# Attention scores as two products of 64 rows side by side, one PSUM bank per head

## The chip, the cores and the metric

The kernel runs on one core of a Trainium2 chip. The metric is device time in microseconds for one execution. On the core, TensorE (PE) multiplies matrices into PSUM, which has eight banks of 512 fp32 columns by 128 partitions; VectorE (DVE), ScalarE (ACT) and GpSimd (POOL) work element by element; transfers are issued from SyncE (SP). The stationary operand of a product is loaded by an instruction of its own (a row of PEld in the profile), then the other operand is streamed through the array (a row of PE).

## The reference

One decoder layer on 256 tokens of width 1024, in fp32. One input projection gives q, k and v for 16 heads of width 64. Heads 0 to 7 are stick-breaking attention, heads 8 to 15 a softmax attention on dilated windows with a bias by distance:

```python
z = jnp.einsum('bhqd,bhkd->bhqk', q_blk, k) * scale        # stick-breaking
log_stay = jnp.where(mask, jax.nn.log_sigmoid(-z), 0.0)
after = lax.cumsum(log_stay, axis=3, reverse=True) - log_stay
w = jnp.where(mask, jnp.exp(jax.nn.log_sigmoid(z) + after), 0.0)
...
sc = jnp.einsum('bhqd,bhqjd->bhqj', q_blk, k_g) * scale    # dilated, three window patterns
sc = sc - slopes_f * dist
p = jnp.exp(sc - m)
```

Each head's output is RMS-normalised with a gain, all heads go through an output projection, then residual and layer norm, a SwiGLU feed-forward part of width 2816, and residual and layer norm again.

## The kernel before

Every fp32 operand of a large product is split into two parts of fp32r, a rounded one (hi) and the rest (lo), by a copy on ScalarE and a subtraction on VectorE; `prod` (L139) forms a product of two split operands as three products, hi hi, hi lo and lo hi, into the same PSUM columns. Weights come in chunks of 1 MB and are split piece by piece (`Weights`, L66; the lines of the copy and of the subtraction are L62 and L63).

The heads are worked in eight pairs j, 0 to 3 stick-breaking, 4 to 7 dilated. `qk_step` projects q and k of a pair transposed, so that the two heads of a pair lie in partitions 0 to 63 and 64 to 127 of one PSUM bank p, q in columns 0 to 255 and k in columns 256 to 511. A pair then runs through these steps (`attend`, L369):

- `evacuate` (L181) brings q and k to SBUF, scaled and split. One of them, q for a stick-breaking pair and k for a dilated one, is padded: 512 columns, of which the first 256 hold head 0 in partitions 0 to 63 and the last 256 head 1 in partitions 64 to 127, with zeros elsewhere. So a product over all 128 rows gives both heads beside each other. The zeros are written once, on GpSimd (L175, L176). Six instructions: two copies and two subtractions of half the partitions for the padded operand (L194, L195), and one of each for the plain one (L197, L198).
- `stick_scores` (L208) computes the transposed scores: keys 0 to 127 against all queries in bank z0 (512 columns, both heads), keys 128 to 255 against queries 128 to 255 in bank z1 (256 columns), three products each, and adds the causal mask by one bf16 product a bank (L217, L218). ScalarE and VectorE form the softplus of the scores in 768 columns and split it (sph, spl).
- `stick_weights` (L233) adds the reverse cumulative sum as products of sph and spl with a triangle (negtri) and with ones (negones), six products at L239, and ScalarE takes the exponential in two instructions (L242 of 512 columns, L243 of 256).
- `dilated_scores` (L248) computes the scores of queries 0 to 127 in s0 (256 columns, both heads) and of queries 128 to 255 in s1 (512 columns), three products each; VectorE adds the bias and takes the maximum (L266), ScalarE the exponential with its sum (L269), VectorE divides.
- `dilated_weights` (L277) transposes them, six products of 128 columns (L281 to L284), and brings 512 columns to SBUF on ScalarE (L287) and 256 on VectorE (L288).
- `values` (L291) multiplies with v in plain fp32. Each head's output has 64 partitions, head 0 in 0 to 63 and head 1 in 64 to 127 of one bank, so these products use 64 columns of the array each. In the trace each of them shows as two passes; those at L298 have 256 columns, those at L303 128.
- `normalise` (L312).

TensorE's program order is written out by `Order` (L332): a clock in estimated microseconds advances with each product with weights (`fill`), each step is due a fixed delay after the step before it (`LAG_A`, `LAG_B`) and has an estimated cost (1.2 for stick-breaking scores, 0.97 for dilated ones), and is put between the products when its time has come. The framework's scheduler orders the instructions of each engine after that by its own estimate of when operands are ready, and can put products of one step apart. PSUM is held as pairs of banks under the names in, big, sml and o.

After the attention come the output projection and the first layer norm, until 140 us, and then the feed-forward part, whose products fill the rest.

## Time and profile before

| | us |
|---|---|
| median of 3 runs | 325.23 |
| lowest and highest run | 324.73 and 325.82 |
| span of the profiled execution | 324.6 |
| TensorE busy in it | 309.9 |
| VectorE, ScalarE busy | 204.7, 177.3 |

The span goes from the first to the last instruction of one profiled execution. The page gives no other time of it; the median of the runs is 0.6 us above the span. Products are pipelined: a PE row's length holds the way through the array too, so rows overlap, and the distance between the starts of two rows is what the first of them takes of the engine. A time in square brackets at a row's end is the engine's idle time before it, with what ended it.

### The profile page before, as it was taken

How to read it: one execution, taken by the hardware profiler on the slowest of the kernel's cores; microseconds unless marked ns; L12 is line 12 of the kernel's file. 1: busy time of each engine (PE TensorE's matmuls, PEld its weight loads, DVE VectorE, ACT ScalarE, POOL GpSimd, SP SyncE). 2: the span in 40 equal slices, each digit the busy share in tenths (PEclk: the TensorE clock that was granted, in tenths of full speed). 3: DMA queues.
4: the chain of work that ended last, by engine and by line, in shares of the span. 5: the costliest groups of instructions: out<-in, count | busy, mean ns of one | idle time of the engine just before them, and what ended most of it. 6: DMA issues, size and time to landing. Idle time of an engine off the chain costs nothing.

```text
span 324.6 us, 5469 instructions
## 1 busy us (share of the span) xinstructions
PE 309.9 (95%) x2168; PEld 283.6 (87%) x2168; DVE 204.7 (63%) x400; ACT 177.3 (55%) x376; POOL 10.6 (3%) x27
## 2 busy tenths in 40 slices
PE   5799999999999999999999999999999999999990
PEld 5688898799997778999999999999999988888890
DVE  3768889867888469997636456464644635250444
ACT  5669899777886547665546364453635543330000
POOL 2010000000000001200000000000000000000102
PEclk9999999999999999999999999999999999999996
DMA  6997876658532203399555464554546365000011
GB/s 182 339 405 280 319 242 239 239 206 333 193 123 73 112 2 129 112 351 383 194 169 221 140 239 142 212 178 164 226 137 240 143 214 175 2 0 0 0 67 65
DMA packets 10809, 58.35 MB, mean 180 GB/s; under 512 B 1312, under 2 KB 2336, under 8 KB 4512
## 3 DMA queue, kind: packets, MB, share of 16 engines
q1 hardware_dynamic: 10784, 58.01, 48.7%
q8 instruction: 17, 0.28, 0.3%
q14 instruction: 8, 0.07, 0.1%
HBM read 56.95 MB, written 1.05 MB: 179 GB/s over the span
## 4 chain that ended last, share of the span: by engine, by line
PE 89%; ACT 3%; DMA 2%; DVE 2%; POOL 1%; SPq 1%; issue 1%; DVEq 0%; POOLq 0%; ACTq 0%
PE pg L142 12%; PE pg L143 12%; PE pg L141 12%; PE p_in L141 7%; PE p_in L143 6%; PE p_in L142 6%; PE d L141 6%; PE d L142 6%; PE d L143 6%; DMA wraw<-in_wqk 2%; PE acc L143 2%; PE acc L141 2%; ACT whi L62 2%; PE acc L142 2%; PE o L298 2%; PE z L239 1%
## 5 line engine op out<-in xcount | busy, mean ns | idle before, releaser
L63 DVE TENSOR_TENSOR wlo<-wraw,whi 128x512 fp32r<-128x512 f32 (+2 forms) x178 | 127.5, 741 | 75.2 <-ACT whi L62 74.8
L62 ACT ACTIVATE whi<-wraw 128x512 fp32r<-128x512 f32 (+2 forms) x178 | 112.8, 668 | 79.5 <-PE pg L142 47.9
L141 PE MATMUL pg<-xhi,whi 128*128 128x256 f32 x304 | 85.5, 281 | 0.0
L143 PE MATMUL pg<-xhi,wlo 128*128 128x256 f32 x304 | 85.4, 281 | 0.0
L142 PE MATMUL pg<-xlo,whi 128*128 128x256 f32 x304 | 85.4, 281 | 0.0
L142 PEld LDWEIGHTS pg<-xlo,whi 128*128 128x128 f32 x304 | 57.4, 189 | 0.0
L141 PEld LDWEIGHTS pg<-xhi,whi 128*128 128x128 f32 x304 | 57.3, 189 | 0.0
L143 PEld LDWEIGHTS pg<-xhi,wlo 128*128 128x128 f32 x304 | 57.3, 189 | 0.0
L141 PE MATMUL p_in<-xhi,whi 128*128 128x256 f32 x128 | 37.2, 293 | 5.4 <-ACT whi L62 5.4
L142 PE MATMUL d<-wlo,a 128*128 128x512 f32 (+1 forms) x110 | 38.3, 348 | 0.0
L141 PE MATMUL d<-whi,a 128*128 128x512 f32 (+1 forms) x110 | 38.3, 348 | 0.0
L143 PE MATMUL d<-whi,a 128*128 128x512 f32 (+1 forms) x110 | 38.2, 348 | 0.0
L143 PE MATMUL p_in<-xhi,wlo 128*128 128x256 f32 x128 | 36.7, 288 | 0.3 <-DVE wlo L63 0.2
L142 PE MATMUL p_in<-xlo,whi 128*128 128x256 f32 x128 | 36.5, 288 | 0.0
L141 PEld LDWEIGHTS p_in<-xhi,whi 128*128 128x128 f32 x128 | 24.9, 195 | 6.7 <-ACT whi L62 5.8
L143 PEld LDWEIGHTS p_in<-xhi,wlo 128*128 128x128 f32 x128 | 24.9, 195 | 0.7 <-DVE wlo L63 0.7
L142 PEld LDWEIGHTS p_in<-xlo,whi 128*128 128x128 f32 x128 | 24.9, 195 | 0.3 <-issue 0.2
L141 PEld LDWEIGHTS d<-whi,a 128*128 128x128 f32 x110 | 20.7, 188 | 2.9
L142 PEld LDWEIGHTS d<-wlo,a 128*128 128x128 f32 x110 | 20.8, 189 | 2.9
L143 PEld LDWEIGHTS d<-whi,a 128*128 128x128 f32 x110 | 20.7, 188 | 2.9
L471 ACT ACTIVATE rs<-mv,eps_ln 128x1 f32<-128x1 f32 x4 | 1.1, 287 | 26.5 <-DVE mv L469 26.5
L141 PE MATMUL pg<-whi,xhi 128*128 128x256 f32 x48 | 13.8, 288 | 0.0
(123 smaller groups left out, 429.0 us busy)
## 6 DMA issues: line engine op xcount, KB each, us to landing
wraw<-in_wgu SPq DMA_DIRECT2D x22, 1024.0 KB, 4.9
wraw<-in_wd SPq DMA_DIRECT2D x11, 1024.0 KB, 4.8
wraw<-in_wqk SPq DMA_DIRECT2D x6, 1024.0 KB, 5.0
wraw<-in_wo SPq DMA_DIRECT2D x4, 1024.0 KB, 4.8
wraw<-in_wv SPq DMA_DIRECT2D x3, 1024.0 KB, 6.6
rows<-in_lnrows SPq DMA_DIRECT2D x2, 1024.0 KB, 5.7
wraw<-in_wqk SPq DMA_DIRECT2D x6, 256.0 KB, 6.6
wraw<-in_wv SPq DMA_DIRECT2D x2, 512.0 KB, 5.8
```

Of the source, the lines that this page charges most:

```text
L62: nc.scalar.activation(hi, src, AF.Copy)
L63: nc.vector.tensor_sub(lo, src, hi)
L141: nc.tensor.matmul(dst, lhs[0], rhs[0], start=start, stop=False, skip_group_check=True)
L142: nc.tensor.matmul(dst, lhs[0], rhs[1], start=False, stop=False, skip_group_check=True)
L143: nc.tensor.matmul(dst, lhs[1], rhs[0], start=False, stop=stop, skip_group_check=True)
L239: nc.tensor.matmul(dst, lhs, rhs, start=False, stop=True, skip_group_check=True)
L298: nc.tensor.matmul(o[r, 0:256], vt[g, 0][:, c], w0[:, h * 256:h * 256 + 256], start=True, stop=False, skip_group_check=True)
L471: nc.scalar.activation(r[:, 0:1], mv[:, 1:2], AF.Ln, bias=eps_ln)
```

## The change

The padded operands and their zeros go. `evacuate` copies q of both heads and k of both heads into one tile of 512 columns (oh, the rest in ol), two copies and two subtractions. The new `by_head` forms the scores of each head from its own 64 partitions, three products (hi hi, hi lo, lo hi) for each of two pieces of columns, the two heads in turn, each into a bank of its own: head 0 into a bank of big, head 1 into one of sml. A bank holds 384 columns: for a stick-breaking head 256 for keys 0 to 127 and 128 for keys 128 to 255, for a dilated head 128 for queries 0 to 127 and 256 for queries 128 to 255. So the products of the scores have 256 and 128 columns where they had 512 and 256. What follows goes by head: the mask is one product a bank on columns 0 to 127 and 256 to 383; `stick_weights` has products of 384 and 128 columns, eight where there were six; the exponentials and the copies of w have 384 columns each; `dilated_scores` goes through one head after the other; `values` reads w by head. The cost of a score step in the order is 1.0 where it was 1.2, and 0.77 where it was 0.97. The lines that are left out change comments alone.

```diff
     nc.gpsimd.tensor_copy(negones, cs[:, 2, :])
     nc.gpsimd.tensor_copy(blkr, blk)
 
-    # per pair: one operand keeps its two heads in separate columns, zero elsewhere
-    padded = []
-    for i in range(2):
-        ph = at.tile([128, 512], F32R, name=f"padhi{i}", bufs=1)
-        pl = at.tile([128, 512], F32R, name=f"padlo{i}", bufs=1)
-        nc.gpsimd.memset(ph.bitcast(F32), 0.0)
-        nc.gpsimd.memset(pl.bitcast(F32), 0.0)
-        padded.append((ph, pl))
-
     mixed = {}
 
     def evacuate(j, p):
-        a_kind = j < 4
-        ph, pl = padded[j % 2]
-        oh = at.tile([128, S], F32R, tag="oh", name="oh")
-        ol = at.tile([128, S], F32R, tag="ol", name="ol")
-        qs = slice(0, 256)
-        ks = slice(256, 512)
-        pc, oc = (qs, ks) if a_kind else (ks, qs)
-        pscale, oscale = (SCALE, 1.0) if a_kind else (1.0, SCALE)
-        for h in range(2):
-            r = slice(h * 64, h * 64 + 64)
-            c = slice(h * 256, h * 256 + 256)
-            nc.scalar.activation(ph[r, c], p[r, pc], AF.Copy, scale=pscale)
-            nc.vector.scalar_tensor_tensor(pl[r, c], p[r, pc], pscale, ph[r, c],
-                                           op0=ALU.mult, op1=ALU.subtract)
-        nc.scalar.activation(oh, p[:, oc], AF.Copy, scale=oscale)
-        nc.vector.scalar_tensor_tensor(ol, p[:, oc], oscale, oh, op0=ALU.mult, op1=ALU.subtract)
-        return (ph, pl), (oh, ol)
-
-    def heads(t, n):
-        return t[:, :2 * n].rearrange("p (h n) -> p h n", h=2)
-
-    def second(t):
-        return t.rearrange("p (h n) -> p h n", h=2)[:, :, 128:256]
-
-    def stick_scores(j, pad, plain):
-        ph, pl = pad
-        oh, ol = plain
-        z0 = bank("big", "z0")
-        z1 = bank("sml", "z1")
-        prod(z0, (oh[:, 0:128], ol[:, 0:128]), (ph, pl), True, True)
-        prod(heads(z1, 128), (oh[:, 128:256], ol[:, 128:256]), (second(ph), second(pl)), True, True)
+        oh = at.tile([128, 512], F32R, tag="oh", name="oh")
+        ol = at.tile([128, 512], F32R, tag="ol", name="ol")
+        for c, scale in ((slice(0, 256), SCALE), (slice(256, 512), 1.0)):
+            nc.scalar.activation(oh[:, c], p[:, c], AF.Copy, scale=scale)
+            nc.vector.scalar_tensor_tensor(ol[:, c], p[:, c], scale, oh[:, c], op0=ALU.mult, op1=ALU.subtract)
+        return oh, ol
+    def by_head(banks, oh, ol, pieces):
+        for dst, lhs, rhs in pieces:
+            for i, (a, b) in enumerate(((oh, oh), (oh, ol), (ol, oh))):
+                for h in range(2):
+                    r = slice(h * 64, h * 64 + 64)
+                    nc.tensor.matmul(banks[h][:, dst], a[r, lhs], b[r, rhs],
+                                     start=dst.start == 0 and i == 0, stop=i == 2, skip_group_check=True)
+    Q, K = 0, 256
+    def stick_scores(j, oh, ol):
+        z = bank("big", "z0"), bank("sml", "z1")
+        by_head(z, oh, ol, ((slice(0, 256), slice(K, K + 128), slice(Q, Q + 256)),
+                            (slice(256, 384), slice(K + 128, K + 256), slice(Q + 128, Q + 256))))
         mb = maskb[:, None, :].to_broadcast([128, 2, 128])
-        z0d = z0.rearrange("p (h n) -> p h n", h=2)
-        nc.tensor.matmul(z0d[:, :, 0:128], identb, mb, start=False, stop=True, skip_group_check=True)
-        nc.tensor.matmul(heads(z1, 128), identb, mb, start=False, stop=True, skip_group_check=True)
         sph = sk.tile([128, 768], F32R, tag="sph", name="sph")
         spl = sk.tile([128, 768], F32R, tag="spl", name="spl")
         ab = at.tile([128, 768], F32, tag="ab", name="ab")
-        parts = ((z0, slice(0, 512), 512), (z1, slice(512, 768), 256))
-        for z, c, n in parts:
-            nc.scalar.activation(ab[:, c], z[:, :n], AF.Abs)
+        for h in range(2):
+            diagonal = z[h].rearrange("p (a n) -> p a n", n=128)[:, 0:3:2, :]
+            nc.tensor.matmul(diagonal, identb, mb, start=False, stop=True, skip_group_check=True)
+        cols = slice(0, 384), slice(384, 768)
+        for h in range(2):
+            nc.scalar.activation(ab[:, cols[h]], z[h][:, :384], AF.Abs)
         nc.scalar.activation(ab, ab, AF.Exp, scale=-1.0)
         nc.scalar.activation(ab, ab, AF.Ln, bias=1.0)
-        for z, c, n in parts:
-            nc.vector.scalar_tensor_tensor(ab[:, c], z[:, :n], 0.0, ab[:, c], op0=ALU.max, op1=ALU.add)
+        for h in range(2):
+            nc.vector.scalar_tensor_tensor(ab[:, cols[h]], z[h][:, :384], 0.0, ab[:, cols[h]],
+                                           op0=ALU.max, op1=ALU.add)
         nc.vector.tensor_copy(sph, ab)
         nc.vector.tensor_sub(spl, ab, sph)
-        return z0, z1, sph, spl
-
-    def stick_weights(z0, z1, sph, spl):
-        z0d = z0.rearrange("p (h n) -> p h n", h=2)
+        return z, sph, spl
+    def stick_weights(z, sph, spl):
         for sp in (sph, spl):
-            s1 = sp[:, 512:768]
-            for dst, lhs, rhs in ((z0, negtri, sp[:, 0:512]), (z0d[:, :, 128:256], negones, heads(s1, 128)),
-                                  (z1[:, :256], negtri, s1)):
-                nc.tensor.matmul(dst, lhs, rhs, start=False, stop=True, skip_group_check=True)
-        w0 = at.tile([128, 512], F32, tag="w0", name="w0")
-        w1 = at.tile([128, 256], F32, tag="w1", name="w1")
-        nc.scalar.activation(w0, z0, AF.Exp)
-        nc.scalar.activation(w1, z1[:, :256], AF.Exp)
-        return w0, w1
+            for h in range(2):
+                s = sp[:, h * 384:h * 384 + 384]
+                nc.tensor.matmul(z[h][:, :384], negtri, s, start=False, stop=True, skip_group_check=True)
+                nc.tensor.matmul(z[h][:, 128:256], negones, s[:, 256:384], start=False, stop=True,
+                                 skip_group_check=True)
+        w = []
+        for h in range(2):
+            w.append(at.tile([128, 384], F32, tag=f"w{h}", name=f"w{h}"))
+            nc.scalar.activation(w[h], z[h][:, :384], AF.Exp)
+        return w
 
     bias_sb = at.tile([128, 8, 256], F32, name="bias_sb", bufs=1)
 
-    def dilated_scores(j, pad, plain):
-        ph, pl = pad
-        oh, ol = plain
-        s0 = bank("sml", "s0")
-        s1 = bank("big", "s1")
-        php = ph.rearrange("p (h n) -> p h n", h=2)
-        plp = pl.rearrange("p (h n) -> p h n", h=2)
-        prod(heads(s0, 128), (oh[:, 0:128], ol[:, 0:128]),
-             (php[:, :, 0:128], plp[:, :, 0:128]), True, True)
-        prod(s1, (oh[:, 128:256], ol[:, 128:256]), (ph, pl), True, True)
+    def dilated_scores(j, oh, ol):
+        s = bank("big", "s0"), bank("sml", "s1")
+        by_head(s, oh, ol, ((slice(0, 128), slice(Q, Q + 128), slice(K, K + 128)),
+                            (slice(128, 384), slice(Q + 128, Q + 256), slice(K, K + 256))))
         e = at.tile([128, 768], F32, tag="ab", name="e")
-        e0, e1 = e[:, 0:256], e[:, 256:768]
         st = at.tile([128, 4, 3], F32, tag="st", name="st")
-        for b, (sc, e, n) in enumerate(((s0, e0, 128), (s1, e1, 256))):
-            for h in range(2):
-                c = slice(h * n, h * n + n)
-                i = 2 * b + h
-                hd = 2 * (j - 4) + h
+        for h in range(2):
+            hd = 2 * (j - 4) + h
+            for b, (o, n) in enumerate(((0, 128), (128, 256))):
+                c = slice(h * 384 + o, h * 384 + o + n)
+                i = 2 * h + b
                 nc.vector.tensor_tensor_reduce(
-                    e[:, c], sc[:, c], bias_sb[:, hd, 256 - n:256], -1.0, 3.0e38,
+                    e[:, c], s[h][:, o:o + n], bias_sb[:, hd, 256 - n:256], -1.0, 3.0e38,
                     ALU.add, ALU.min, st[:, i, 0:1])
                 nc.scalar.activation(e[:, c], e[:, c], AF.Exp, bias=st[:, i, 0:1], scale=-1.0,
                                      accum_out=st[:, i, 1:2])
-            nc.vector.reciprocal(st[:, 2 * b:2 * b + 2, 2:3], st[:, 2 * b:2 * b + 2, 1:2])
-            for h in range(2):
-                c = slice(h * n, h * n + n)
-                nc.vector.tensor_scalar(e[:, c], e[:, c], st[:, 2 * b + h, 2:3], None, op0=ALU.mult)
-        return e0, e1
-
-    def dilated_weights(e0, e1):
-        t0 = bank("big", "t0")
-        t1 = bank("sml", "t1")
-        for h in range(2):
-            nc.tensor.transpose(t0[:, h * 256:h * 256 + 128], e0[:, h * 128:h * 128 + 128], ident)
-        for h in range(2):
-            nc.tensor.transpose(t0[:, h * 256 + 128:h * 256 + 256], e1[:, h * 256:h * 256 + 128], ident)
-            nc.tensor.transpose(t1[:, h * 128:h * 128 + 128], e1[:, h * 256 + 128:h * 256 + 256], ident)
-        w0 = at.tile([128, 512], F32, tag="w0", name="w0")
-        w1 = at.tile([128, 256], F32, tag="w1", name="w1")
-        nc.scalar.activation(w0, t0, AF.Copy)
-        nc.vector.tensor_copy(w1, t1[:, :256])
-        return w0, w1
-
-    def values(j, w0, w1):
+            nc.vector.reciprocal(st[:, 2 * h:2 * h + 2, 2:3], st[:, 2 * h:2 * h + 2, 1:2])
+            for b, (o, n) in enumerate(((0, 128), (128, 256))):
+                c = slice(h * 384 + o, h * 384 + o + n)
+                nc.vector.tensor_scalar(e[:, c], e[:, c], st[:, 2 * h + b, 2:3], None, op0=ALU.mult)
+        return e
+    def dilated_weights(e):
+        w = []
+        for h in range(2):
+            t = bank(("big", "sml")[h], f"t{h}")
+            for i in range(3):
+                c = slice(h * 384 + i * 128, h * 384 + i * 128 + 128)
+                nc.tensor.transpose(t[:, i * 128:i * 128 + 128], e[:, c], ident)
+            w.append(at.tile([128, 384], F32, tag=f"w{h}", name=f"w{h}"))
+            if h == 0:
+                nc.scalar.activation(w[h], t[:, :384], AF.Copy)
+            else:
+                nc.vector.tensor_copy(w[h], t[:, :384])
+        return w
+    def values(j, w):
         g, pj = divmod(j, 4)
         o = bank("o", "o")
         for h in range(2):
             c = slice(pj * 128 + h * 64, pj * 128 + h * 64 + 64)
             r = slice(h * 64, h * 64 + 64)
-            nc.tensor.matmul(o[r, 0:256], vt[g, 0][:, c], w0[:, h * 256:h * 256 + 256],
+            nc.tensor.matmul(o[r, 0:256], vt[g, 0][:, c], w[h][:, 0:256],
                              start=True, stop=False, skip_group_check=True)
         for h in range(2):
             c = slice(pj * 128 + h * 64, pj * 128 + h * 64 + 64)
             r = slice(h * 64, h * 64 + 64)
-            nc.tensor.matmul(o[r, 128:256], vt[g, 1][:, c], w1[:, h * 128:h * 128 + 128],
+            nc.tensor.matmul(o[r, 128:256], vt[g, 1][:, c], w[h][:, 256:384],
                              start=False, stop=True, skip_group_check=True)
         sq = at.tile([128, S], F32, tag="sq", name="sq")
         nc.scalar.activation(sq, o[:, :S], AF.Square)
...
     od = Order()
 
     def attend(j, p):
         a_kind = j < 4
-        pad, plain = evacuate(j, p)
+        oh, ol = evacuate(j, p)
         scores, weigh = (stick_scores, stick_weights) if a_kind else (dilated_scores, dilated_weights)
         lags = LAG_A if a_kind else LAG_B
 
         def step1():
-            x1 = scores(j, pad, plain)
+            x1 = scores(j, oh, ol)
 
             def step2():
-                x2 = weigh(*x1)
+                x2 = weigh(*x1) if a_kind else weigh(x1)
 
                 def step3():
-                    x3 = values(j, *x2)
+                    x3 = values(j, x2)
                     od.after(lags[3], 0.43, lambda: normalise(j, *x3))
                 od.after(lags[2], 0.68, step3, lambda: v_at.get(j // 4, 1e9) <= od.now)
             od.after(lags[1], 0.9 if a_kind else 0.65, step2)
-        od.after(lags[0], 1.2 if a_kind else 0.97, step1)
+        od.after(lags[0], 1.0 if a_kind else 0.77, step1)
 
     vt, v_at = {}, {}
 
```

## Rows read from the trace of the kernel before

**Rows 1.** The page's first part: busy time, share of the span, instructions.
```profile
PE 309.9 (95%) x2168; PEld 283.6 (87%) x2168; DVE 204.7 (63%) x400; ACT 177.3 (55%) x376; POOL 10.6 (3%) x27
```

**Rows 2.** Busy time by stretch: stretch, its length, each engine, clock, DMA.
```profile
17.00:45.00 28.00, 27.72 (x171) 23.19 (x170) 22.10 (x39) 24.02 (x51) 0.67 (x3) 1.00 0.85 317
...
140.00:312.00 172.00, 172.00 (x1264) 163.35 (x1263) 91.50 (x152) 73.88 (x139) 1.74 (x3) 1.00 0.45 164
```

**Rows 3.** Instructions in order of time, TensorE, scores of pair 3: start, length.
```profile
56.92 0.40 PE L141 MATMUL z<-padhi,oh 128*128 128x512 f32 x1
...
57.62 0.27 PE L141 MATMUL z<-padhi,oh 128*128 128x256 f32 x1
57.73 0.28 PE L142 MATMUL z<-padlo,oh 128*128 128x256 f32 x1
...
57.97 0.28 PE L217 MATMUL z<-maskb,identb 128*128 128x256 bf16 x1
```

**Rows 4.** The same view, stick weights of pair 2, first product and what follows.
```profile
61.00 0.40 PE L239 MATMUL z<-sph,negtri 128*128 128x512 f32 x1
...
61.95 0.39 PE L141 MATMUL p_in<-whi,xhi 128*128 128x512 f32 x1
```

**Rows 5.** The same view, value products of pair 1 and their neighbours.
```profile
40.71 0.28 PE L143 MATMUL p_in<-xhi,wlo 128*128 128x256 f32 x1
40.83 0.28 PE L141 MATMUL p_in<-xhi,whi 128*128 128x256 f32 x1
41.04 0.65 PE L298 MATMUL o<-w,v 128*64 128x256 f32 x4
41.52 0.39 PE L303 MATMUL o<-w,v 128*64 128x128 f32 x4
41.84 0.39 PE L142 MATMUL p_in<-xlo,whi 128*128 128x256 f32 x1
42.07 0.28 PE L143 MATMUL p_in<-xhi,wlo 128*128 128x256 f32 x1
```

**Rows 6.** The same view, weight loads behind those value products and at a mask.
```profile
41.84 0.19 PEld L142 LDWEIGHTS p_in<-xlo,whi 128*128 128x128 f32 x1 [0.17 <-issue]
41.95 0.19 PEld L143 LDWEIGHTS p_in<-xhi,wlo 128*128 128x128 f32 x1
...
57.97 0.10 PEld L217 LDWEIGHTS <-identb 128*128 128x128 bf16 x1
```

**Rows 7.** The same view, ScalarE, VectorE and TensorE at pair 0's evacuation.
```profile
17.93 0.38 ACT L194 ACTIVATE padhi<-p_in 64x256 fp32r<-64x256 f32 x1 [2.09 <-PE p_in L143]
18.87 0.38 ACT L194 ACTIVATE padhi<-p_in 64x256 fp32r<-64x256 f32 x1 [0.56 <-DVE padlo L195]
19.93 0.38 ACT L197 ACTIVATE oh<-p_in 128x256 fp32r<-128x256 f32 x1
...
18.42 0.42 DVE L195 SCALAR_TENSOR_TENSOR padlo<-p_in,padhi 64x256 fp32r<-64x256 f32 x1 [1.85 <-ACT padhi L194]
...
19.90 0.28 PE L143 MATMUL p_in<-xhi,wlo 128*128 128x256 f32 x1
20.46 0.47 PE L141 MATMUL z<-padhi,oh 128*128 128x512 f32 x1 [0.28 <-ACT oh L197]
```

**Rows 8.** The same view, w and value products of pair 6, scores of pair 7.
```profile
100.75 0.60 ACT L287 ACTIVATE w<-t 128x512 f32<-128x512 f32 x1
...
101.22 0.42 DVE L288 COPY w<-t 128x256 f32<-128x256 f32 x1
...
101.41 0.65 PE L298 MATMUL o<-w,v 128*64 128x256 f32 x4 [0.21 <-ACT w L287]
101.89 0.38 PE L303 MATMUL o<-w,v 128*64 128x128 f32 x2
102.20 0.39 PE L141 MATMUL s<-padhi,oh 128*128 128x256 f32 x1
...
104.40 0.51 PE L143 MATMUL s<-padhi,ol 128*128 128x256 f32 x2
```

## The prediction

> **What bounds the kernel now.** I read the busy line first, then the busy time by stretch, then TensorE's instructions in order of time, then the other engines where TensorE waits. TensorE is busy 95% of the span [rows 1]. By stretch it is busy 27.72 of 28.00 us from 17 to 45 and 172.00 of 172.00 from 140 to 312, at the full clock; VectorE and ScalarE are near their limit only early (22.10 and 24.02 of 28.00) and have half their time free later [rows 2]. So from 17 us on the end is set by how long TensorE's stream of products takes: a microsecond taken from it is a microsecond of the span, and what VectorE or ScalarE lose counts only where TensorE stands and waits for them. The 17 us ahead of that are arrival and splitting of inputs, which the change doesn't touch.
>
> **What a product costs.** A busy PE row isn't its price; the distance from start to start is. In the scores of pair 3 three products of 512 columns start at 56.92 and end their turn at 57.62, 0.233 each; those of 256 follow every 0.117 [rows 3]. That is 0.456 ns a column, with each weight load under the product before it.
>
> **Scores (by_head).** Before, a pair has three products of 512 and three of 256: 56.92 to 57.97, 1.05 us [rows 3]. Afterwards there are twelve instructions, two beside each other in six steps: three of 256 columns and three of 128. If the halves of the array run side by side, streaming is 3 x 0.117 + 3 x 0.058 = 0.53, half of before. That they do has one near case in the trace: the value products split the array by columns. Both heads' four last passes take 41.52 to 41.84, 0.32 [rows 5]; in pair 6 one head's two passes alone take 101.89 to 102.20, 0.31 [rows 8]. The second head costs nothing. I take this for the split by rows too.
>
> The same rows show the toll. From the last full product ahead of the value products to their first is 0.21 (40.83 to 41.04), where 0.117 is usual: 0.09 lost [rows 5]. On the way back the last passes of 0.107 each would be over at 41.73, yet the next product starts at 41.84, and the one behind it 0.23 later instead of 0.117: another 0.10 and 0.11. The weight loads say why: with nothing to hide under, two loads of 128 columns start at 41.84 and 41.95, 0.108 apart [rows 6]. So entering costs 0.09 and one bare load, 0.108; leaving costs 0.10 and one bare load. Behind stick-breaking scores comes the mask, whose bf16 load is half as long (0.10 against 0.19 [rows 6]), so I take 0.05 there.
>
> The Trainium skill (TensorEngine Tiling (Array Packing), Key Properties) says that a change of tiling mode drains TensorE, in whichever direction the array is split. That is what the rows show for the split by columns; if it did not hold by rows, the third rival below would be the result.
>
> A short step doesn't reach 0.058. The next pair of weights (64 rows, 128 columns) must be in place, and the only bare loads of 128 columns are 0.108 apart. No row has a load of 64 rows: from below it is 0.05 (half the elements), from above 0.108; I take 0.108, the row with as many columns, and with the start some 0.115. The Trainium skill (TensorE: Matmul & The Clock Gate, LDWEIGHTS (loading the stationary operand)) states that a load's time follows the columns and not the rows, 128 / 1.2 = 107 ns by its formula; the 0.108 agrees for the full height. By the opposite reading, loads by elements, the fourth rival is the result. From far above, a step of 128 columns costs as much as an fp32 one, two passes of 0.107: 0.21.
>
> Sum of a pair: 0.09 + 0.108 + 3 x 0.117 + 2 x 0.115 + 0.058 + 0.10 = 0.94, with the load on leaving 1.05 for a dilated pair and 0.99 for a stick-breaking one. Before 1.05: a gain of 0 and of 0.06. Over four pairs of each kind **-0.25 us** for a halved stream.
>
> **Stick weights.** Before, six products of 2048 columns in all: 61.00 to 61.95, 0.95 us [rows 4]. Afterwards eight, four of 384 and four of 128 at full height, in turn with two different weights. Columns are the same, but under a product of 128 (0.058) the next load of 0.108 has no room: four steps of 0.115 and four of 0.175 are 1.16, 0.21 more. Over four pairs **+0.85 us** (from below 0, from above 4 x (0.21 - 0.058) x 4 = +2.4). Mask, transposes and value products keep their columns.
>
> **Evacuation.** Six instructions become four: one ScalarE copy of some 0.38 and one VectorE subtraction of some 0.43 go, in each of 8 pairs. Most of it lies under TensorE's stream and is worth nothing; where TensorE waited it counts. For pair 0 the chain runs ScalarE 17.93, VectorE 18.42, ScalarE 18.87 and, last, ScalarE 19.93, and the scores start at 20.46, where the product before them, started at 19.90, left off at 20.02 [rows 7]. With q and k of both heads in one copy each, the second copy ends near 19.25 and its rest near 19.71, before 20.02. **-0.44 us**, from below 0 where TensorE's order keeps another wait there. The four cleared buffers on GpSimd go too; the inputs hadn't landed then, so nothing.
>
> **Evacuating w, and splits of a step.** w is now 384 columns on each engine where it was 512 and 256, and both heads' first value products need it: the head-1 product now waits for VectorE's copy, or in a stick-breaking pair for ScalarE's second. Behind that product in TensorE's queue stand all later products. For most pairs both copies end before it. In pair 6 TensorE already waits 0.21 for ScalarE's (started at 100.75) and begins at 101.41, while VectorE's starts at 101.22 and at some 0.55 would end near 101.77 [rows 8]. ScalarE's ends 0.12 earlier, head 1 starts up to 0.36 later: **+0.1**, between -0.1 and +0.4. Second, the order puts products of a step apart when a part comes late: pair 7 starts its scores at 102.20 and brings the last products at 104.40 [rows 8]. That was free; now each extra visit costs the toll of about 0.35. The shorter evacuation makes such splits rarer, pair 1 in the crowded start may keep one: **+0.3**, between 0 and +1.
>
> The order's cost for a score step falls by 0.2, so its estimated time runs ahead of the real one by more than before. Delays are counted from the end of a step and filled with the same products, so I take nothing; a shift of one product, 0.1 to 0.2, is its bound either way.
>
> **Sum.** -0.25 + 0.85 - 0.44 + 0.1 + 0.3 = +0.56 us, on a span of 324.6. The runs give 325.23 as median, 0.6 over the profiled span, between 324.73 and 325.82; the same distance kept, the changed kernel stands at 325.8.
>
> **Rivals.**
> First, slower: a product of 128 columns costs as much as the fp32 one, 0.21. For: the groups of instructions by shape hold no product of two fp32r parts under 256 columns, so its price is open upwards. Against: operand and instruction are the same as at 256. It is 0.35 more for each of 8 score steps (2 x 0.1 + 0.15) and 1.5 more over the stick weights: +4.3, 330.1 us. It decides from a distance of about 0.14 on.
> Second, slower too, the change doesn't do what it says: the halves load or run one after the other. Then six steps of 0.23 and the toll: +0.7 a pair, 331.4. Against it the two heads of the value products [rows 5, 8].
> Third, faster: the split by rows needs no drain and its loads are hidden. The toll of 0.41 (dilated) and 0.35 goes: -3.0, 322.8 us. For it: no row has this split. Against: the toll stands at each of the value steps. The Trainium skill (TensorEngine Tiling (Array Packing), Theoretical Speedup) gives up to twice the rate for half the rows; no run here shows it, and this is the rival that comes nearest.
> Fourth, faster: short loads by elements, so short steps at 0.06, but the toll stays. Scores save another 8 x 0.16 (two steps and the bare load), and if loads of full height also hide better than I think the weights lose nothing, -0.85: 323.7 us.
>
> **How the numbers follow.** What this kernel's runs can tell from no change is about 0.3%, 1 us. Forecast 0.42 (its own range 324.6 to 327.0, so 0.34 within, 0.06 slower, 0.02 faster); first rival 0.14; second 0.08; third 0.19; fourth 0.17, of which 0.13 faster and 0.04 within. Faster 0.34, within 0.38, slower 0.28. The range goes from the third to the first rival, 322.8 to 330.1, and leaves out the second and some of the third.
>
> **What would show it.** Right: the two heads' score products start within a few ns of each other; the first of a step comes 0.2 after the product before; steps of 128 stand about 0.115 apart; eight stick-weight products take 1.16; no gap at 20.02. Wrong: steps of 128 at 0.06 or at 0.21, the heads 0.117 apart, or a first score product 0.117 behind its predecessor. A TensorE gap at the value products of a dilated pair would be a wait that I priced too low.

## The result, and the profile after

The changed kernel takes 327.95 us (median of nine runs, 326.29 to 329.34) against 325.32 us (nine runs, 324.73 to 328.31): a ratio of 1.0067, 95% interval 1.0041 to 1.0093. Repeated, it was 327.17 against 325.88, 1.0044 (1.0023 to 1.0065). So it is slower by about half a per cent. The forecast was 325.8 in 322.8 to 330.1: the time lies in the range, but above the 324.6 to 327.0 that the forecast gave to its own case, and "slower" had only 0.28. In some executions of either kernel TensorE has half its clock for 3.4 us early on (last section), some 2 us longer; of the runs with a mean granted clock of 0.991 or more the medians are 326.89 (17 runs) and 325.34 (66, one execution of 784 us left out), 1.55 us apart.

The profiled executions hide this: both spans are 324.6 us. Wherever an execution has both on record, its time stands 1.7 to 2.1 us above its span. So 324.6 belongs to some 326.5 us: for the kernel before more than any of the three runs that the forecast started from, for the changed kernel the second lowest of nine (326.51). The 0.6 us that the forecast kept between span and median lie between different executions; as it adds its difference to the median, its 325.8 doesn't depend on them. The busy line and the windows of the changed kernel, to be set beside [rows 1, 2], say no more: TensorE is full, VectorE and ScalarE lost work that nobody waited for.
```profile
PE 310.2 (96%) x2224; PEld 283.1 (87%) x2224; DVE 201.2 (62%) x392; ACT 173.0 (53%) x368; POOL 8.7 (3%) x23
```
```profile
17.00:45.00 28.00, 27.68 (x182) 22.66 (x181) 22.66 (x40) 24.74 (x52) 0.92 (x4) 1.00 0.90 340
140.00:312.00 172.00, 172.00 (x1274) 163.34 (x1273) 92.66 (x154) 74.19 (x140) 1.74 (x3) 1.00 0.47 167
```
What to look at is the second count: in the same 172 us the changed kernel runs 1274 products, the one before 1264, and nothing of that stage was edited. Cut at the starts of products that both kernels have, three profiles of each (us):

| stretch | before | changed | difference |
|---|---|---|---|
| last projection product of 256 columns ahead of pair 0's scores to pair 4's first score | 58.43 to 58.48 | 59.60 to 59.70 | +1.2 |
| from there to the first feed-forward product by channel | 68.46 to 68.48 | 68.46 to 68.51 | 0.0 |
| from there to the first product of the down projection | 108.43 to 108.45 | 107.27 | -1.2 |
| from there to the end | 69.38 to 69.40 | 69.40 to 69.41 | 0.0 |

The stick-breaking pairs lose 1.2 us, the dilated pairs nothing on balance, and in these profiles the feed-forward stage gives back as much by a pace of its own (last section).

The edited operations are much as forecast. Scores of pair 3 in TensorE's order of time (start, length; x2 are the two heads), answering [rows 3]:
```profile
57.10 0.40 PE L143 MATMUL p_in<-whi,xlo 128*128 128x512 f32 x1
57.42 0.39 PE L187 MATMUL z<-oh 64*128 64x256 f32 x2
57.65 0.28 PE L187 MATMUL z<-ol,oh 64*128 64x256 f32 x2
57.77 0.28 PE L187 MATMUL z<-oh,ol 64*128 64x256 f32 x2
57.88 0.23 PE L187 MATMUL z<-oh 64*128 64x128 f32 x2
57.94 0.28 PE L187 MATMUL z<-ol,oh 64*128 64x128 f32 x2
58.05 0.28 PE L187 MATMUL z<-oh,ol 64*128 64x128 f32 x2
58.27 0.39 PE L203 MATMUL z<-maskb,identb 128*128 128x256 bf16 x2
58.41 0.48 PE L141 MATMUL p_in<-whi,xhi 128*128 128x512 f32 x1
```
The heads share a step; the way in costs 0.09 (57.10 + 0.23 to 57.42), the second step comes 0.23 behind the first, and a step of 256 columns takes 0.117. Of the steps of 128 the first takes 0.06 (57.88 to 57.94), the second 0.11 (57.94 to 58.05), and 0.21 pass between the last step and the mask. The weight loads of these steps start 0.11 to 0.12 apart, the bare ones at the head of the visit (57.42, 57.53) and those of the short steps (57.77 to 57.99):
```profile
57.42 0.19 PEld L187 LDWEIGHTS z<-oh 64*128 64x128 f32 x2 [0.37 <-issue]
57.53 0.19 PEld L187 LDWEIGHTS z<-ol,oh 64*128 64x128 f32 x2
...
57.77 0.19 PEld L187 LDWEIGHTS z<-oh 64*128 64x128 f32 x2
57.88 0.20 PEld L187 LDWEIGHTS z<-ol,oh 64*128 64x128 f32 x2
57.99 0.20 PEld L187 LDWEIGHTS z<-oh,ol 64*128 64x128 f32 x2
```
From the second step on, each load starts while the step ahead of its own runs, and never less than 0.11 behind the load before. So the first short step can end with its columns, and the next one takes 0.11: the price of a short product falls on the product behind it. Stick weights of pair 2, answering [rows 4], show the same. They take 61.30 to 62.39, 1.09 us. Each product of 128 columns takes 0.06, a product of 384 takes 0.17 at the head of the run and 0.23 behind one of 128, and the projection product behind the run takes 0.29 (62.39 to 62.69):
```profile
61.30 0.33 PE L220 MATMUL z<-sph,negtri 128*128 128x384 f32 x1
61.47 0.22 PE L221 MATMUL z<-sph,negones 128*128 128x128 f32 x1
61.53 0.39 PE L220 MATMUL z<-sph,negtri 128*128 128x384 f32 x1
61.76 0.22 PE L221 MATMUL z<-sph,negones 128*128 128x128 f32 x1
61.82 0.39 PE L220 MATMUL z<-spl,negtri 128*128 128x384 f32 x1
...
62.33 0.22 PE L221 MATMUL z<-spl,negones 128*128 128x128 f32 x1
62.39 0.45 PE L141 MATMUL p_in<-whi,xhi 128*128 128x512 f32 x1
62.69 0.39 PE L142 MATMUL p_in<-wlo,xhi 128*128 128x512 f32 x1
```
In the kernel before, the product behind the run takes 0.23, from 61.95 [rows 4] to
```profile
62.17 0.40 PE L142 MATMUL p_in<-wlo,xhi 128*128 128x512 f32 x1
```
What the forecast priced too low is in the extracts that follow. Pair 0's scores come in four visits, each with its own way in and out; the gap of [rows 7] is gone, but the first visit is for one product:
```profile
19.93 0.40 PE L141 MATMUL p_in<-whi,xhi 128*128 128x512 f32 x1
20.25 0.38 PE L187 MATMUL z<-oh 64*128 64x256 f32 x1
20.57 0.50 PE L142 MATMUL p_in<-wlo,xhi 128*128 128x512 f32 x1
20.90 0.40 PE L143 MATMUL p_in<-whi,xlo 128*128 128x512 f32 x1
```
From 19.93 to 20.57 is 0.64 where a product of 512 takes 0.23, and the one behind it takes 0.33: 0.51 for one score product. All operands of pair 0 had been in place since 19.46, the end of VectorE's second subtraction, so it is the order made ahead of the run that splits this step, and not a late operand:
```profile
19.04 0.42 DVE L178 SCALAR_TENSOR_TENSOR ol<-p_in,oh 128x256 fp32r<-128x256 f32 x1 [0.45 <-ACT oh L177]
```
And pair 7, answering [rows 8]: ScalarE's second copy waits its turn behind two weight splits, TensorE stands, and the visit is broken off after two products:
```profile
100.34 0.37 ACT L177 ACTIVATE oh<-p_in 128x256 fp32r<-128x256 f32 x1
100.60 1.15 ACT L62 ACTIVATE whi<-wraw 128x512 fp32r<-128x512 f32 x2
101.74 0.38 ACT L177 ACTIVATE oh<-p_in 128x256 fp32r<-128x256 f32 x1
```
```profile
101.04 0.49 PE L293 MATMUL o<-sqh,blkr 128*128 128x256 f32 x2
102.18 0.33 PE L187 MATMUL s<-oh 64*128 64x128 f32 x2 [0.65 <-ACT oh L177]
102.70 0.50 PE L141 MATMUL acc<-whi,mh 128*128 128x512 f32 x1 [0.19 <-DVE ol L178]
...
104.26 0.33 PE L187 MATMUL s<-ol,oh 64*128 64x128 f32 x2
```

### The profile page after: what moved, and what is told of

Its sections match the earlier page's. It is cut to its first block, busy times and chain, and to the rows that moved or that the text cites. A ratio compares the mean times of both kernels' runs of the same rounds, so it can differ in the third digit from the quotient of the medians.

```text
span 324.6 us, 5556 instructions
## 1 busy us (share of the span) xinstructions
PE 310.2 (96%) x2224; PEld 283.1 (87%) x2224; DVE 201.2 (62%) x392; ACT 173.0 (53%) x368; POOL 8.7 (3%) x23
## 4 chain that ended last, share of the span: by engine, by line
PE 84%; ACT 5%; DVE 4%; DMA 2%; issue 1%; POOL 1%; SPq 1%; DVEq 0%; POOLq 0%
PE pg L142 12%; PE pg L143 12%; PE pg L141 12%; PE d L141 6%; PE d L142 6%; PE d L143 6%; PE p_in L141 6%; PE p_in L142 6%; PE p_in L143 6%; ACT whi L62 2%; DMA wraw<-in_wqk 2%; PE acc L141 2%; PE acc L143 2%; PE acc L142 2%; PE o L275 1%
## 5 line engine op out<-in xcount | busy, mean ns | idle before, releaser
L141 PE MATMUL p_in<-xhi,whi 128*128 128x256 f32 x128 | 38.1, 299 | 4.6 <-ACT whi L62 4.6
```

The costliest lines, as they stand in the source:

```text
L141: nc.tensor.matmul(dst, lhs[0], rhs[0], start=start, stop=False, skip_group_check=True)
```

## Experiments

**Both kernels again, and with the order held.** The first two kernels are unchanged. In the other two every TensorE instruction of the attention keeps the order of the program:
```diff
+    def mm(*args, **kw):
+        i = nc.tensor.matmul(*args, **kw)
+        return tc.keep_in_program_order(i) if pinned[0] else i
...
-                    nc.tensor.matmul(banks[h][:, dst], a[r, lhs], b[r, rhs],
+                    mm(banks[h][:, dst], a[r, lhs], b[r, rhs],
```


> The kernel before, unchanged, timed against itself: it shows how far two timings of one program lie apart, and gives a second profile of it. Theory: the ratio is 1.000 within 0.3%, and the feed-forward part, whose products the change doesn't touch, differs between two profiles of the same program by up to 1 us (256-column products at 117.3 or at 118.7 ns). Rival: the feed-forward part of this program always runs at 118.7 ns, and the changed kernel's at 117.3, so that the change has a hand in it.

> The changed kernel, unchanged, timed again. Theory: 1.1 us of loss lies ahead of the feed-forward part, from 17 us to its first product by channel, and the time is 1.003 to 1.008 of before. Rival: the difference of the first timing was the state of the chip; then the ratio is 1.000 within 0.3% here.

> The kernel before with the same edit: TensorE's attention instructions held in written order. Theory: here a split of a score step needs no switch of the array and costs nothing, so the edit gives at most the 0.4 us gap ahead of pair 0's scores and the 0.1 to 0.3 of a split value step: between -0.7 and +0.3 us. Rival: holding the order is worth as much here as in the changed kernel (1 us or more); then the splits, and not the switching, are what costs.

> The changed kernel, with TensorE's instructions of the attention stage held in the order in which the program writes them, so that no score step is put apart (the first two projections are left free). Theory: in the changed kernel pair 0's scores come in five visits and pair 7's in two; each extra visit costs some 0.35 us of switching and bare weight loads, and pair 7 stands 0.8 us before it. Held together, three to four visits go: 1.0 to 1.8 us faster than the changed kernel, near the kernel before. Rival: the split products are free as they were before the change, and what costs is the narrow products; then holding the order costs up to 0.5 us where TensorE now waits for late operands.

The repeats gave 325.89 (ratio to the kernel before 1.0016, 0.9989 to 1.0042) and 327.17 (1.0044). Held in order, the kernel before took 331.2 (1.0157), 5.3 us more than free, and the changed one 330.48 (1.0153), 3.3 us more. Both expectations failed. Pair 0's scores now stand behind the 24 products of the value projection and start at 28 to 29 us, and at the output projection TensorE stands for the evacuation of pair 7, 3.35 us in the kernel before and 2.75 in the changed one. Behind that the granted clock is 0.57 from 105 to 109 us in both, and products of 512 columns start 0.43 apart instead of 0.23. The kernel before:
```profile
105.49 0.77 PE L61 MATMUL acc<-whi,mh 128*128 128x512 f32 x1 [3.35 <-DVE ol L207]
106.05 0.63 PE L61 MATMUL acc<-wlo,mh 128*128 128x512 f32 x1
```
That the changed kernel loses 2 us less agrees with splits that cost it something and the other nothing, but beside waits of this size it doesn't show it.

**Each half of the change alone.** The line that chooses, in `attend`, for the first; `not a_kind` for the second:
```diff
+        by = a_kind
+        q, k = evacuate(j, p) if by else evacuate_pad(j, p)
```


> Pairs 0 to 3 as in the changed kernel, pairs 4 to 7 as in the kernel before (with one set of padded operands in place of two). Theory (short products and visits cost TensorE time in these pairs): pairs 4 to 7 begin their scores 0.7 to 1.1 us later than in the kernel before (79.0 to 79.4 us against 78.3), and that stands to the start of the feed-forward stage; the time is 326.6 to 327.0 us against 325.9. Rival (the loss sits in pair 7's late operands, the stick pairs wait for weights anyway): the shift dissolves before the feed-forward stage and the time is within 0.3 us of before. A second question: products of the feed-forward stage have been 118.7 ns apart in every profile of a kernel of the before kind and 117.3 ns in every one of the after kind; if that belongs to the stick half, this one shows 117.3 and the stage is 1.2 us shorter.

> Pairs 0 to 3 as in the kernel before, pairs 4 to 7 as in the changed kernel (their operands lie in the buffers of the padded ones). Theory (pair 7's scores begin after two products, with a wait for their operands of 0.81 us and another visit): the start of pair 4's scores within 0.1 us of the kernel before, the feed-forward stage begins 0.3 to 0.6 us later; time 326.2 to 326.5 us against 325.9. Rival (all the loss is in the stick pairs): within 0.2 us of before. Second question as for the other half: 118.7 or 117.3 ns between the products of the feed-forward stage.

The stick half: 328.36 (ratio 1.0088, 1.006 to 1.0116). Its six runs include five with the early half clock (the sixth took 325.95), so its time overstates it; its profile puts 59.17 us between first score and pair 4's first score, as the changed kernel does (59.17 to 59.25; before 57.87 to 57.91), and nothing dissolves behind it (68.44 to the feed-forward products). By the profile the rival is out. The dilated half: 325.77 (1.0023, 0.9997 to 1.0049), a time that leaves both open; that stretch is 57.96, as before, and the next one 68.50 against 68.46 to 68.48. The loss expected there, 0.3 to 0.6, is not in the profile: pair 7 does cost TensorE 0.3 more, and pairs 4 to 6 give 0.2 back. So by the profiles the loss is the stick-breaking half.

**The late operand first, and the visits glued.** The products of a step are reordered so that the first one needs what is evacuated last; in the second kernel the scores of pairs 0 and 1 are also taken up at once:
```diff
-            for i, (a, b) in enumerate(((oh, oh), (oh, ol), (ol, oh))):
+            for i, (a, b) in enumerate(parts):
...
-        od.after(lags[0], 1.0 if a_kind else 0.77, step1)
+        od.after(lags[0] if j > 1 else 0.0, 1.0 if a_kind else 0.77, step1)
```


> The changed kernel with the product that needs the operand evacuated last at the head of each score step. TensorE's order is that of the changed kernel but for pair 7, whose scores stand in one visit behind six products of the output projection. Theory (a visit begun too early waits for its operands and pays its way in twice): pairs 0 to 3 as in the changed kernel (pair 4's scores begin at 79.1 to 79.5 us), 0.5 to 1.0 us less behind pair 7; time 326.2 to 326.7 us against 327.2. Rival (the operands come late in any order, ScalarE and VectorE set it): the wait only moves, within 0.2 us of the changed kernel.

> As the one before, and the scores of pairs 0 and 1 taken up as soon as their operands are there, each pair in one visit instead of five and two. Theory (each visit of a score step costs 0.2 to 0.35 us of TensorE): pair 4's scores begin 0.8 to 1.4 us earlier than in the changed kernel (77.9 to 78.5 us); time 325.2 to 326.0 us. Rival (TensorE waits for the split weights in that stage anyway, so the visits fill holes): pair 4's scores begin within 0.3 us of 79.2 us, and the time is that of the one before, 326.4 us; with the scores' wait for their operands in front of it, up to 0.5 us later.

Late operand first: 326.37 (1.0056, 1.003 to 1.0082). By the profile the stretch from pair 4's scores to the feed-forward products by channel is 68.13 us instead of 68.46 to 68.51: 0.35 less, short of the 0.5 expected. Most of the wait only moved, to a product of the output projection that needs pair 7's bank:
```profile
103.09 0.40 PE L142 MATMUL acc<-wlo,mh 128*128 128x512 f32 x1
104.18 0.50 PE L141 MATMUL acc<-whi,mh 128*128 128x512 f32 x1 [0.69 <-DVE ol L178]
```
Glued: 326.54 (1.0032, 1.001 to 1.0053), no better than without. Pair 4's first score came 74.53 us behind the first product, against 74.61 to 75.36 in the changed kernel and 73.50 to 74.35 before: the 0.8 to 1.4 us are not there. Cut as in the table it is 59.59, against 59.60 to 59.70 in the changed kernel, so the rival holds. TensorE's order of time shows what was traded. Pair 1's single visit waits 0.85 for its operands, and later a projection product waits for a weight that VectorE splits late, behind the attention:
```profile
20.95 0.39 PE L143 MATMUL p_in<-whi,xlo 128*128 128x512 f32 x1
22.18 0.39 PE L187 MATMUL z<-oh,ol 64*128 64x256 f32 x2 [0.85 <-DVE ol L178]
...
28.36 0.50 PE L142 MATMUL p_in<-wlo,xhi 128*128 128x512 f32 x1 [0.50 <-DVE wlo L63]
```
In this stage the visits fill holes that are there in the other order too: what the tolls took, the waits take.

**Short products widened.**
```diff
-                nc.tensor.matmul(z[h][:, 128:256], negones, s[:, 256:384], start=False, stop=True,
+                nc.tensor.matmul(z[h][:, 128:384], negones, s[:, 128:384], start=False, stop=True,
...
-                            (slice(256, 384), slice(K + 128, K + 256), slice(Q + 128, Q + 256))))
+                            (slice(256, 512), slice(K + 128, K + 256), slice(Q + 128, Q + 384))))
```


> The changed kernel with every short product of 128 columns of the score steps and of the stick weights widened to 256 columns (into columns that are not used, or with values that do not belong there: scores and weights are wrong). Theory (a short step waits for the load of the next weights, 0.108 to 0.11 us, so its columns are free up to there): pair 2 and 3's score visits 1.08 to 1.15 us against 1.08, their eight stick-weight products 1.09 to 1.2 us against 1.09. Rival (streaming sets a short step): three short steps and four short products at 0.058 more each, 1.25 and 1.32 us.

The first score piece of the dilated pairs is widened in the same way. Pair 3's scores in TensorE's order of time, then pair 2's stick weights:
```profile
56.37 0.40 PE L143 MATMUL p_in<-whi,xlo 128*128 128x512 f32 x1
...
57.15 0.28 PE L187 MATMUL z<-oh 64*128 64x256 f32 x2
57.27 0.28 PE L187 MATMUL z<-ol,oh 64*128 64x256 f32 x2
57.38 0.28 PE L187 MATMUL z<-oh,ol 64*128 64x256 f32 x2
57.59 0.39 PE L203 MATMUL z<-maskb,identb 128*128 128x256 bf16 x2
57.74 0.47 PE L141 MATMUL p_in<-whi,xhi 128*128 128x512 f32 x1
```
```profile
60.62 0.34 PE L220 MATMUL z<-sph,negtri 128*128 128x384 f32 x1
60.80 0.28 PE L221 MATMUL z<-sph,negones 128*128 128x256 f32 x1
...
61.81 0.42 PE L141 MATMUL p_in<-whi,xhi 128*128 128x512 f32 x1
62.07 0.41 PE L142 MATMUL p_in<-wlo,xhi 128*128 128x512 f32 x1
```
Twice the columns cost 0.06 over three steps (57.10 to 58.41 became 56.37 to 57.74), all of it in the first short step (0.06 became 0.117), and 0.06 over four products and the one behind them (61.30 to 62.69 became 60.62 to 62.07), where streaming would add 0.17 and 0.23. The load of the next weights paces the short products, as forecast, but for the first short step of a visit, which its columns set. The one run took 324.64 us, less than any of the changed kernel: its other lengths moved the order, and the visit with pair 7's first two products takes 1.30 us by the count of the next section instead of 2.23, transposes and normalising products ahead of it included (from pair 4's scores to the feed-forward products 67.58 us). In this one profile, where a visit falls is worth as much as the arithmetic.

**A version meant to beat both, and the unchanged kernels a third time.** The old stick half, the dilated half by head with the late operand first, and
```diff
             nc.scalar.activation(oh[:, c], p[:, c], AF.Copy, scale=scale)
+        for c, scale in ((slice(0, 256), SCALE), (slice(256, 512), 1.0)):
             nc.vector.scalar_tensor_tensor(ol[:, c], p[:, c], scale, oh[:, c], op0=ALU.mult, op1=ALU.subtract)
```


> Pairs 0 to 3 as in the kernel before; pairs 4 to 7 by head, with the product that needs the operand evacuated last at the head of each score step, and both ScalarE copies of an evacuation ahead of both VectorE subtractions. Theory (by head the dilated pairs cost TensorE 0.2 us less a pair, and only pair 7's split gave it back; pair 7's bank is given back some 0.4 us sooner): from pair 4's first score to the first transpose of the normalised rows 45.4 to 45.9 us, against 46.26 in the kernel before and 45.91 in the changed kernel with the late product first; the time 0.3 to 0.9 us under the kernel before. Rival (that stretch is bound by the weights that ScalarE and VectorE split, so what TensorE saves comes back as a wait): 46.2 us, and the time of the kernel before.

> The kernel before, unchanged, for the distance between products of the feed-forward stage. If it belongs to the run, any kernel shows 118.7 or 117.3 ns, and this one may show 117.3; if it belongs to the program, it is 118.7 ns for the third time and the stage from the first product by channel to the first of the down projection takes 108.43 us again.

> The changed kernel, unchanged, for the same question: 117.3 ns for the third time and 107.27 us for that stage if it belongs to the program, either value if it belongs to the run. The attention up to the feed-forward stage takes 1.1 to 1.4 us longer than in the kernel before, whichever it is.

It took 326.0 against 325.94, ratio 0.9988 (0.9959 to 1.0017): not to be told from the kernel before. Its profile has the 0.35 us (68.11 us from pair 4's scores to the feed-forward products, 68.46 to 68.48 before), the same as the late operand alone; putting the copies first added nothing. The third runs (326.45 before, 325.92 changed; one each) belong to the feed-forward pace, last section.

## Why the prediction was right, and where not

**The mechanism was right.** The halves run side by side: the two heads start 2 to 4 ns apart in the steps of 256 columns, so the second rival is out. The toll is there, 0.09 on the way in and a second step 0.23 behind the first, so the third is out. Bare loads of 64 rows start 0.11 apart like those of 128, and the second short step takes 0.11, so the fourth is out. No short step comes near 0.21, so the first is out.

**Scores in one visit (-0.06 a stick-breaking pair, 0 a dilated one): right, slightly better.** From way in to mask it is 0.93, where 0.94 was worked out, but by two errors that cancel: the first short step took 0.06 and not 0.115, and from the last step to the mask 0.21 passed and not 0.16. Counted from the start of the last projection product ahead to the next one behind, less its 0.23, pairs 2 and 3 went from 1.18 and 1.20 to 1.08 and 1.08: -0.11 each, since the bare load that was priced at the mask doesn't show. Pairs 4 to 6 came to -0.08, +0.02 and -0.15; the last goes straight on to value products, and the way out of the scores shows no price there.

**Stick weights (+0.21 a pair, +0.85): right for a pair that runs by itself, too large in sum.** Pair 2 went from 0.94 to 1.09, and the product behind it from 0.23 to 0.29: +0.21. Pair 3 came to +0.23. Pairs 0 and 1 now run one behind the other, with a wait of 0.32 for spl between them where the kernel before had other products and a split visit of value products; weights and values together, they cost 0.19 more. That makes +0.63.

**Evacuation (-0.44): the gap went, the gain did not arrive.** Pair 0's first score now follows its predecessor, of 512 columns, by 0.32, where it followed one of 256 by 0.56: 0.09 lost instead of 0.44. But it is one product, and three more visits of pair 0 follow.

**Splits (+0.3): the step that failed.** Pairs 0 and 1 were to cost 0.56 less (evacuation and scores), and all splits together 0.3 more. By the same count their scores went from 3.00 to 3.19 us, and the delays of the products behind a visit from 0.15 to 0.37: +0.42. Pair 7 adds 0.33. A visit for one score product took 0.51, 0.4 more than the product and not 0.35. Above all, the forecast said that a shorter evacuation makes splits rarer: the order is made from estimated times, and pairs 0 and 1 kept their five visits together (two and three before, now four and one), pair 7 its two. At full height their splits had cost next to nothing, 0.07 behind pair 0's first visit. In the glued kernel the tolls could not be had back there.

**The wait for w (+0.1 at pair 6): right in kind, at another place.** Pair 6's value products now run behind pair 7's scores and wait for nothing. It was pair 3's second head that waited for ScalarE's second Exp: its values took 1.14 instead of 0.89, +0.25.

Summed: -0.22 for the scores of pairs 2 and 3, +0.63, +0.42, +0.25 and 0.09 for the way in to pair 4's scores, which the cut puts into this stretch, make the 1.2 us that the stick-breaking stretch lost. In the dilated one -0.21, less that 0.09, and +0.33 end near nothing, and 68.46 to 68.51 is what the table shows. The forecast of +0.56 had the right sign and half the size of what the attention lost.

**What stays open:** by the profiles the feed-forward stage gives back 1.2 us and the two kernels would be even; the timed runs, which leave no trace, are 1.55 us apart. Two numbers on record speak against the give-back in them. The median span of the runs at the full clock is 323.5 us before and 325.0 changed, so the profiled executions (324.0 to 324.6 of either kernel) lie above the median of the one and below that of the other. And the changed kernel with its late operand first has the slower pace in its profile (last section), yet against the kernel before on its chip it loses 0.8 us at the full clock (326.01 against 325.20), the changed kernel 1.3 (326.89 against 325.56). The attention alone would make that 0.9 and 1.2, with the pace it would be 0.9 and 0.0. These are medians of runs that spread over 2 us. What the runs of one program differ by no trace shows: three profiles of the kernel before lie within 0.6 us, its runs at the full clock between 324.32 and 326.96.

## What to carry to other kernels

Halving the streamed columns buys little where the next weight load sets the step: here a second step of 128 columns cost 0.11 where one of 256 cost 0.117, and what a short stick-weight product saved came back in the product behind it. So count a run of short products up to the product behind it. Count the visits to a tiling mode and not only the products in one, at 0.4 us more for a visit of one step in this kernel, and ask which operand of a visit comes last. Cut two profiles at products that both have before believing that equal spans mean an equal kernel, and look where the profiled execution stands among the timed ones.

## What the hardware showed beyond that

**A pace that goes with the program, in the profiles.** The feed-forward products of 256 columns are 118.7 ns apart in one program and 117.3 in another, though these instructions are the same. TensorE from 150 to 250 us (products in brackets, then clock, DMA share, GB/s) in the kernel before, the changed one, and the changed one with the late operand first:
```profile
150.00:250.00 100.00, 100.00 (x845) 1.00 0.54 193
```
```profile
150.00:250.00 100.00, 100.00 (x854) 1.00 0.56 198
```
```profile
150.00:250.00 100.00, 100.00 (x845) 1.00 0.55 199
```
All three profiles of the kernel before show 118.7, all three of the changed one 117.3. That it belongs to the run is not what they say. Nor does it follow the kind of scores: 117.3 in the stick half, the widened and the order-held changed kernel; 118.7 in the dilated half, the last version, the order-held kernel before, and the changed kernel with its late operand first, glued or not. Each program but these two was profiled once. Why one program gets 1.2 us less in that stage is open, and so is whether its timed runs do.

**The clock may fall early.** The last version's and the kernel before's stretch from 12 to 16 us (third run of the latter), granted clock 0.57 and 1.00:
```profile
12.00:16.00 4.00, 3.89 (x19) 3.69 (x20) 3.43 (x6) 3.29 (x6) 0.00 (x0) 0.57 1.02 355
```
```profile
12.00:16.00 4.00, 3.89 (x33) 3.69 (x32) 3.69 (x6) 3.79 (x6) 0.00 (x0) 1.00 1.00 358
```
For 3.4 us TensorE has 1.2 GHz instead of 2.4 and runs 19 products instead of 33; pair 0's first score comes at 22.05 us instead of 20.34. What made it fall isn't shown: from 8 to 12 us TensorE was busy 2.81 of 4 us there and 2.16 here. A mean granted clock of 0.990 or less, which I take for its mark, is found in 13 of 79 executions of the kernel before and 5 of 22 of the changed one, so a comparison of half a per cent needs more than a handful of runs.
